# Pair 5 of the MLP with seven products, two more kept items at heads 14 to 16, and the odd tile's conv ahead of the last gate step

## The chip, the cores and the metric

The kernel runs on one core of a Trainium2 chip. The metric is device time in microseconds, the median of three runs; lower is better. Profiles are of one further execution, whose own time stands beside its span, since the span counts from the first to the last instruction only.

The engines are TensorE (PE; its weight loads are listed apart as PEld), VectorE (DVE), ScalarE (ACT), GpSimd (POOL) and SyncE (SP, which here only issues DMAs). Each takes its instructions in a fixed order and waits at one whose input is not there yet.

## The reference

One layer of a decoder trunk on 512 rows of 1024 in fp32: attention with forget gates (16 heads of 64), layernorm, a gated MLP with a causal three-tap convolution on the gate, layernorm, and a gated per-layer embedding.

```
mix = fox_mixer(x, w_in, b_f, w_out)          # 16 heads, scores + c_q - c_k, softmax, w_out
x = layer_norm(ALPHA * x + mix, g, b)
u, g = split(x @ w_up, [2816])                # 1024 -> 2 x 2816
g = causal_dwconv(g, conv_w, conv_b)          # 3 taps along the sequence
x = layer_norm(ALPHA * x + (gelu(g) * u) @ w_down, g2, b2)
x = x + sigmoid(x @ w_gate + b_gate) * (p @ w_proj)
```

## The kernel before

**Products.** Every fp32 product is three matmuls of a rounded type (`three`, L152): high part times high part, high times low, low times high. Activations and weights are cut into these parts: ACT makes `whi` (L123), DVE makes `wlo` as the difference (L129). Weights come in units of 512 KB (128 x 1024) through SyncE's queue into `raw`, a ring of four buffers; the parts are five deep.

**Attention.** A loop over h runs scores of head h, transposes of the probabilities of head h − 1 (`turn`) and values of head h − 2 (`values`: L593 on PE, then ACT L599 and DVE L600 write `o`; behind an odd head ACT L602 and DVE L603 make the parts `oh` and `ol`). The output product starts early: `out_first(k)` adds row block k into the banks `ao`, for half of the columns, and the other half goes into the banks `ap` after the loop. A scheduler sets the order on each engine here, by its own estimate of times.

**Layernorm.** For each of four row tiles DVE adds `ao` and `ap` to `y` (L689), takes statistics and normalizes (L705, L706); PE transposes the result (`nt`, L714).

**MLP.** The 22 column tiles f of the up product are taken in pairs j = 0 to 10 (f = 2j and 2j + 1), gate g and value u of each. A plain tile takes 24 matmuls of 512 columns for g and 24 for u. In the pairs of `UP_PAIRS` the 2 x 2 block product is done with seven half-size products instead of eight (Strassen's scheme in Winograd's form): `up_step` has four stages, with 24, 24, 24 and 12 matmuls of 256 columns for each of g and u. The stages collect in `E`, from which the convolution (`conv`: ACT, then two DVE operations), gelu and the product with u follow. Between the steps of a pair the down product of an earlier part runs in pieces (`between`). In the MLP the order on DVE and ACT is the order in which the code is written (`manual_schedule`); an instruction that waits holds up what stands behind it there.

**Kept sums.** A seven-product pair needs sums of weight blocks. For the pairs in `KEPT` they are made during attention: `keep_load` (L478) loads two 512 KB pieces, `ka` into a buffer of its own (one only) and `kb` into the ring `raw`; `keep_sums` (L489 to L492, four DVE subtractions) makes the sums in place; the next `keep_load` stores them to DRAM (`kept`, L472) before it loads the next item. One item is one side (u or g) of one pair: eight items for the four pairs. From `kept` the MLP loads them like weights.

**Operands.** The sums and parts of a pair's result, which the down product reads, are made at the pair's end or, for a pair whose successor is in `APART`, inside the successor's first step (`operand_sums`, L885 to L888; `operand_parts`, L893 and L894).

Of the kernel before, what the change touches and what calls it, by code (L numbers as in the profile page):

```python
# [17 lines left out]
S = 512  # L18
D = 1024
H = 16  # L20
# [10 lines left out]

CHUNKS = (None, (1,) * 12, (1,) * 12, (2, 1) * 4)

UP_PAIRS = (2, 3, 4, 6, 7, 9)

KEPT = (3, 4, 6, 7)

DMA_PAIRS = (1, 2)

APART = (2, 3, 4, 7)  # L40
HALF = S // 2
ALPHA = 2.0 ** 0.25
EPS = 1e-5
# [99 lines left out]
def trunk_layer(ctx: ExitStack, tc: tile.TileContext, xT, x2d, pT, w0, wqk, wv1, wv2, bf, wo, wup, cwb,  # L143
# [323 lines left out]
    def keep_load():  # L467

        if made:
            to, ab = made.pop()  # L470
            for n, t in enumerate(ab):
                nc.sync.dma_start(to[:, 2 * n:2 * n + 2, :], t.rearrange("p (a b) -> p a b", b=512))  # L472
        if to_keep:
            (j, q), to = to_keep.pop(0)
            ab = (ap.tile([P, UNIT], F32, name=f"ka{j}_{q}", tag="keep", bufs=1),
                  base.tile([P, UNIT], F32, name=f"kb{j}_{q}", tag="raw", bufs=RAW_BUFS))
            for n, t in enumerate(ab):
                nc.sync.dma_start(t.rearrange("p (a b) -> p a b", b=P), wup[2 * j + n, 1 - q])  # L478
            in_work.append((to, ab))
# [166 lines left out]
    for h in range(H + 2):  # L646
        m, s = divmod(h, 2)
        if h == 2:
            project(2, 0)
        if h < H:  # L650
            scores(h)

            if s == 0 and h != 2:
                keep_sums()
                keep_load()
        if m + 1 < KD and h != 2:
            project(m + 1, s)
        for k in OUT_FIRST.get(h, ()):
            out_first(k)
        if s == 1 and h + 1 < H:  # L660
            stack(h + 1)
        if 1 <= h < H + 1:
            turn(h - 1)
        if h >= 2:
            values(h - 2)
        if s == 1 and h + 1 < H:
            stack(h + 2)
        if h == H:
            y = base.tile([P, NT, D], F32, tag="xh", name="y")
            for t in range(NT):  # L670
                nc.sync.dma_start(y[:, t, :], x2d[t * P:(t + 1) * P, :])
# [113 lines left out]
    def conv(f):  # L785

        pg = ups.pop((f, 0))
        a = gates[f] = hpool.tile([P, S], F32, tag="a", name=f"a{f}", bufs=2)
        nc.scalar.activation(a, pg, AF.Identity, bias=cw[:, f, 3:4], scale=cw[:, f, 2:3])
        nc.vector.scalar_tensor_tensor(a[:, 1:], pg[:, :S - 1], cw[:, f, 1:2], a[:, 1:],  # L790
                                       op0=ALU.mult, op1=ALU.add)
        nc.vector.scalar_tensor_tensor(a[:, 2:], pg[:, :S - 2], cw[:, f, 0:1], a[:, 2:],
                                       op0=ALU.mult, op1=ALU.add)

    def product(f, e):
        a = gates[f]
        nc.scalar.activation(a, a, AF.Gelu)
        nc.vector.tensor_mul(e, gates.pop(f), ups.pop((f, 1)))
# [67 lines left out]
            del ups[j, s]  # L866
            nc.scalar.activation(e[:, HALF:S], x, AF.Copy)

    def conv_product(fs, E):

        for f in fs:
            c = slice(f % 2 * S, f % 2 * S + S)
            ups[f, 0], ups[f, 1] = E[:, 2 * S:][:, c], E[:, c]
            conv(f)
        for f in fs:
            product(f, E[:, f % 2 * S:f % 2 * S + S])

    def operand_sums(E):

# [63 lines left out]
    for part in range(4):  # L943
        ops = []
        slots = iter(CHUNKS[part] or ())

        def between():
            for _ in range(next(slots, 0)):
                next(before)

        for f in range(6 * part, min(6 * part + 6, NF)):
            q, j = f % 2, f // 2
            if f >= 6:
                next(beside)
            if f == 2:

                ordered.enter_context(tc.manual_schedule(
                    engines={mybir.EngineType.DVE, mybir.EngineType.Activation}))
            if q == 0 and j not in APART:
                E = hpool.tile([P, 8 * HALF], F32, tag="E", name=f"E{j}")  # L960
            if f == 0:
                a, b = slice(0, HALF), slice(HALF, S)
                up(0, 0, a)
                up(0, 1, a)
                up(1, 0, a, (3, x1h, x1l, xt))
                up(0, 0, b)
                up(0, 1, b)
                up(1, 0, b)
                conv(0)
                product(0, E[:, :S])  # L970
                continue
            if j in UP_PAIRS:
                if q == 0:
                    up_step(j, 0, 0, E)
                    between()
                    up_step(j, 0, 1, E, (lambda: operand_sums(E)) if j in APART else None)
                    if j in APART:
                        operand_parts(pending.pop(), E)
                        E = hpool.tile([P, 8 * HALF], F32, tag="E", name=f"E{j}")
                    between()  # L980
                    continue
                for st in (1, 2):
                    up_step(j, st, 0, E)
                    up_step(j, st, 1, E)
                    if st == 1:
                        between()
                between()
                up_step(j, 3, 0, E)
                up_step(j, 3, 1, E)
                conv_product((f, f - 1), E)  # L990
            else:
                if f > 1:
                    up(f, 0)

                n = 4 * (j - 3 * part) + 2 * q
                late = part and any(sum(CHUNKS[part][:n], i) % 3 == 2 for i in range(CHUNKS[part][n]))
                if not late:
                    conv(f)
                between()
                if late:  # L1000
                    conv(f)
                up(f, 1)
                product(f, E[:, q * S:(q + 1) * S])
            if f == 1:
                x_sums()
            if q:
                if part < 3:
                    ops.append([cut_tiles("A", 2, 3, f"a{j}"), cut_tiles("B", 1, 5, f"b{j}", pool=hpool),
                                cut_tiles("S", 4, 4, f"s{j}")])
                    if j + 1 in APART:  # L1010
                        pending.append(ops[-1])
                    else:
                        operand_sums(E)
                        operand_parts(ops[-1], E)
                else:
                    h, l = cut_tiles("S", 4, 4, f"s{j}")
                    e = E[:, :2 * S].rearrange("p (a b) -> p a b", b=HALF)
                    last_cut[:] = [nc.scalar.activation(h, e, AF.Copy).ins]
                    nc.vector.tensor_sub(l, e, h.bitcast(F32))
                    ops.append((h, l))  # L1020
            if j not in UP_PAIRS:
                between()
        if part < 3:
            before = down(part, ops)
# [216 lines left out]
```

## Time and profile before

| | before |
|---|---|
| time, median of 3 runs | 646.02 us (645.39 to 646.28) |
| profiled execution | 645.37 us, span 643.5 us, granted clock 1.000 |
| PE, PEld | 638.3 us (99%), 560.6 us (87%) |
| DVE | 532.4 us (83%) |
| ACT | 383.4 us (60%) |
| POOL | 127.6 us (20%) |
| moved by DMA | 121.08 MB, mean 188 GB/s |

By stage, the end of attention runs from about 196 to 222 us, the first layernorm to about 254, pairs 2 to 5 of the MLP end at about 311.9, 343.0, 374.1 and 403.0 us, pair 9 at 530.6. "Busy" is time in which an instruction runs on the engine; the chain that ended last is the sequence of instructions, followed back from the last one, each of which released the next.

### The profile page before, as it was taken

To read this page: it belongs to the slowest core of one execution; us is meant where nothing else is said; L and a number is where in the kernel's file an instruction comes from. 1 tells how busy PE (TensorE), PEld (TensorE's weight loads), DVE (VectorE), ACT (ScalarE), POOL (GpSimd) and SP (SyncE) were. 2 spreads that over 40 slices of the span, in tenths; PEclk is the share of its full clock that TensorE was granted. 3 is DMA by queue.
4 is the path that set the end of the run, shared out by engine and by line. 5 is a ranking of instruction groups with operands and counts; after the bars stand their busy time and mean duration, and the time that the engine had idled before them with its cause. 6 is when DMAs were issued, how large, how long until landed. Compare 5 with 4: busy or idle time off the path is not lost.

```text
span 643.5 us, 10085 instructions
## 1 busy us (share of the span) xinstructions
PE 638.3 (99%) x3635; PEld 560.6 (87%) x3635; DVE 532.4 (83%) x863; ACT 383.4 (60%) x682; POOL 127.6 (20%) x147
## 2 busy tenths in 40 slices
PE   9999999999999999999999999999999999999997
PEld 7899888888888889989999988999988998888886
DVE  6576778988888599857899987889897998699997
ACT  6274777877785326945757563647555455336872
POOL 2000554454456043110000010101011001002001
PEclk9999999999999999999999999999999999999999
DMA  8763625454588387684676838765746764782732
GB/s 314 249 226 117 209 80 185 160 189 155 177 272 321 129 256 215 135 215 156 202 221 158 227 125 250 192 205 149 238 132 202 193 217 115 164 276 61 232 109 98
DMA packets 49393, 121.08 MB, mean 188 GB/s; under 512 B 4864, under 2 KB 7936, under 8 KB 49344
## 3 DMA queue, kind: packets, MB, share of 16 engines
q1 hardware_dynamic: 44400, 107.21, 49.8%
q0 software_dynamic: 4800, 13.11, 11.0%
q8 instruction: 28, 0.46, 0.3%
q14 instruction: 21, 0.17, 0.1%
q10 hardware_dynamic: 144, 0.13, 0.1%
HBM read 107.72 MB, written 18.87 MB: 197 GB/s over the span
## 4 chain that ended last, share of the span: by engine, by line
PE 97%; DMA 1%; DVE 1%; ACT 0%; issue 0%; SPq 0%; DVEq 0%
PE g L152 18%; PE u L152 18%; PE pp L152 14%; PE x L152 8%; PE pv L152 7%; PE pl L152 7%; PE z L152 4%; PE r L152 3%; PE ap L152 3%; PE o L593 3%; PE t L580 2%; PE ao L152 2%; PE y L152 2%; PE s L543 2%; PE s L545 2%; DMA y<-x2d 1%
## 5 line engine op out<-in xcount | busy, mean ns | idle before, releaser
L123 ACT ACTIVATE whi<-raw 128x1024 fp32r<-128x1024 f32 (+4 forms) x136 | 128.1, 945 | 95.0 <-PE pv L152 17.9
L129 DVE TENSOR_TENSOR wlo<-raw,whi 128x1024 fp32r<-128x1024 f32 (+4 forms) x131 | 140.0, 1076 | 27.9 <-ACT whi L123 27.2
L567 POOL TENSOR_SCALAR pr<-pr,rl 128x128 f32<-128x128 f32 (+1 forms) x64 | 75.5, 1194 | 128.1 <-DVE rl L563 125.6
L281 POOL COPY neghalf<-neghalf 128x1 f32<-128x1 f32 x16 | 9.0, 563 | 247.1 <-ACT neghalf L280 247.1
L152 PE MATMUL g<-x1h,whi 128*128 128x256 f32 (+1 forms) x168 | 54.7, 325 | 0.0
L152 PE MATMUL g<-x1l,whi 128*128 128x256 f32 (+1 forms) x168 | 54.4, 324 | 0.0
L152 PE MATMUL g<-x1h,wlo 128*128 128x256 f32 (+1 forms) x168 | 54.3, 324 | 0.0
L152 PE MATMUL u<-x1l,whi 128*128 128x256 f32 (+1 forms) x160 | 52.9, 331 | 0.0
L152 PE MATMUL u<-x1h,wlo 128*128 128x256 f32 (+1 forms) x160 | 52.9, 331 | 0.0
L152 PE MATMUL u<-x1h,whi 128*128 128x256 f32 (+1 forms) x160 | 52.9, 331 | 0.0
L152 PE MATMUL pp<-xh,whi 128*128 128x512 f32 (+1 forms) x130 | 50.7, 390 | 0.0
L152 PE MATMUL pp<-xl,whi 128*128 128x512 f32 (+1 forms) x130 | 50.7, 390 | 0.0
L152 PE MATMUL pp<-xh,wlo 128*128 128x512 f32 (+1 forms) x130 | 50.5, 390 | 0.0
L559 ACT ACTIVATE pr<-s,nm 128x128 f32<-128x128 f32 (+1 forms) x64 | 33.5, 527 | 9.1 <-DVE nm L555 8.9
L152 PEld LDWEIGHTS g<-x1h,whi 128*128 128x128 f32 x168 | 31.9, 190 | 3.4 <-issue 0.7
L152 PEld LDWEIGHTS g<-x1l,whi 128*128 128x128 f32 x168 | 31.9, 190 | 2.7
L152 PEld LDWEIGHTS g<-x1h,wlo 128*128 128x128 f32 x168 | 31.9, 190 | 2.6
L152 PEld LDWEIGHTS u<-x1l,whi 128*128 128x128 f32 x160 | 30.4, 190 | 3.0
L152 PEld LDWEIGHTS u<-x1h,whi 128*128 128x128 f32 x160 | 30.4, 190 | 3.0
L152 PEld LDWEIGHTS u<-x1h,wlo 128*128 128x128 f32 x160 | 30.4, 190 | 2.8
L123 ACT ACTIVATE whi<-side 128x512 fp32r<-128x512 f32 (+1 forms) x33 | 25.5, 782 | 10.4 <-PE u L152 3.6
L555 DVE CUSTOM_DVE_ANT_0 s<-s,mask 128x128 f32<-128x128 f32 (+1 forms) x64 | 30.1, 510 | 1.7 <-PE s L545 1.5
(636 smaller groups left out, 1870.9 us busy)
## 6 DMA issues: line engine op xcount, KB each, us to landing
raw<-wup SPq DMA_DIRECT2D x34, 512.0 KB, 9.1
raw<-wdn SPq DMA_DIRECT2D x23, 512.0 KB, 6.7
raw<-wqk SPq DMA_DIRECT2D x14, 512.0 KB, 5.8
ka<-wup SPq DMA_DIRECT2D x8, 512.0 KB
kb<-wup SPq DMA_DIRECT2D x8, 512.0 KB, 4.3
kept<-kb SPq DMA_DIRECT2D x8, 512.0 KB, 3.2
kept<-ka SPq DMA_DIRECT2D x8, 512.0 KB
raw<-wo SPq DMA_DIRECT2D x8, 512.0 KB, 4.9
```

What stands on the lines that cost most here:

```text
L123: self.nc.scalar.activation(hi[:, c:e], piece, AF.Copy)
L129: self.nc.vector.tensor_sub(lo[:, c:e], piece, hi[:, c:e].bitcast(F32))
L152: nc.tensor.matmul(ps, lhsT, rhs, start=start and n == 0, stop=stop and n == 2, skip_group_check=on)
L281: with tc.issue_after(nc.gpsimd.tensor_copy(small[:, m + 32:m + 33], small[:, m:m + 1]).ins):
L543: nc.tensor.matmul(ps[:, :n], QA[:, q], KA[:, :n], start=True, stop=False)
L545: nc.tensor.matmul(ps[:, :n], qb[0:68, q], kb[0:68, :n], start=False, stop=True)
L555: last_mask[:] = [nc.vector.tensor_tensor_reduce(ps[:, :w], ps[:, :w], mask[:, S - w:], -1.0, BIG, op0=ALU.add, op1=ALU.min, accum_out=nm[ ...
L559: nc.scalar.activation(pr[:, off:off + w], ps[:, :w], AF.Exp, bias=nm[:, i:i + 1], scale=-1.0, accum_out=ls[:, i:i + 1])
L567: nc.gpsimd.tensor_scalar_mul(pr[:, off:off + w], pr[:, off:off + w], rl[:, i:i + 1])
L580: nc.tensor.transpose(ps[:, w:w + P], pr[:, o:o + P], ident)
L593: nc.tensor.matmul(ps[:, q0:], V[:, j, h], p[:, o:o + w], start=j == 0 and n == 0, stop=j == NT - 1 and n == 1)
```

## The change

Pair 5 becomes a seven-product pair and a kept one: with it the pairs 2 to 7 are consecutive. Pairs 5 and 6 join `APART`, so that the operand sums and parts of pairs 4 and 5 are made inside the first step of pairs 5 and 6. Ten items are now kept; the calls that were made at h = 14 and before are joined by one pair of calls at h = 15 and one at h = 16, so that pair 7's two sides come last, behind pair 5's and 6's. And in every seven-product pair the function that did conv of both tiles and then the product of both is split: the odd tile's conv is written ahead of the gate's last step, its product behind it, then comes the value's last step, then conv and product of the even tile.

```diff
-UP_PAIRS = (2, 3, 4, 6, 7, 9)
-KEPT = (3, 4, 6, 7)
+UP_PAIRS = (2, 3, 4, 5, 6, 7, 9)
+KEPT = (3, 4, 5, 6, 7)
-APART = (2, 3, 4, 7)
+APART = (2, 3, 4, 5, 6, 7)
@@ the loop over h
-            if s == 0 and h != 2:
+            if s == 0 and h != 2 or h == H - 1:
                 keep_sums()
                 keep_load()
+        elif s == 0:
+            keep_sums()
+            keep_load()
@@
-    def conv_product(fs, E):
-        for f in fs:
-            c = slice(f % 2 * S, f % 2 * S + S)
-            ups[f, 0], ups[f, 1] = E[:, 2 * S:][:, c], E[:, c]
-            conv(f)
-        for f in fs:
-            product(f, E[:, f % 2 * S:f % 2 * S + S])
+    def conv_of(f, E):
+        c = slice(f % 2 * S, f % 2 * S + S)
+        ups[f, 0], ups[f, 1] = E[:, 2 * S:][:, c], E[:, c]
+        conv(f)
+    def product_of(f, E):
+        product(f, E[:, f % 2 * S:f % 2 * S + S])
@@ the end of a seven-product pair
                 between()
+                conv_of(f, E)
                 up_step(j, 3, 0, E)
+                product_of(f, E)
                 up_step(j, 3, 1, E)
-                conv_product((f, f - 1), E)
+                conv_of(f - 1, E)
+                product_of(f - 1, E)
```

The lines below L650 move down by three. On DVE, at the end of attention (`o_2241` and `o_2381` are the outputs of the last two pairs of heads, `PTl` low parts of probabilities), there stood before:

```order
343 L600 TENSOR_TENSOR o_2241<-o_2322,o_2241 64x512
344 L603 TENSOR_TENSOR ol<-o_2241,oh 128x512
345 L584 TENSOR_TENSOR PTl_396<-t_0_2353,PTh_394 128x512
346 L584 TENSOR_TENSOR PTl_396<-t_1_2360,PTh_394 128x384
347 L584 TENSOR_TENSOR PTl_396<-t_3_2366,PTh_394 128x384
348 L600 TENSOR_TENSOR o_2381<-o_2372,o_2381 64x512
349 L129 TENSOR_TENSOR wlo_2514<-raw_2405,whi_2513 128x1024
350 L600 TENSOR_TENSOR o_2381<-o_2419,o_2381 64x512
```

And now (`ka_0`, `kb_0` are the item of pair 7's side 0, `ka_1`, `kb_1` that of side 1; the two outputs are named `o_2247` and `o_2403`):

```order
342 L489 TENSOR_TENSOR ka_0_2181<-kb_0_2182,ka_0_2181 128x512
343 L600 TENSOR_TENSOR o_2247<-o_2338,o_2247 64x512
344 L490 TENSOR_TENSOR kb_0_2182<-kb_0_2182 128x512
345 L129 TENSOR_TENSOR wlo_2524<-raw_2361,whi_2523 128x1024
346 L491 TENSOR_TENSOR kb_0_2182<-kb_0_2182,ka_0_2181 128x512
347 L603 TENSOR_TENSOR ol<-o_2247,oh 128x512
348 L492 TENSOR_TENSOR ka_0_2181<-ka_0_2181,kb_0_2182 128x512
...
352 L600 TENSOR_TENSOR o_2403<-o_2394,o_2403 64x512
353 L129 TENSOR_TENSOR wlo_2536<-raw_2427,whi_2535 128x1024
354 L489 TENSOR_TENSOR ka_1_2285<-kb_1_2286,ka_1_2285 128x512
355 L600 TENSOR_TENSOR o_2403<-o_2441,o_2403 64x512
```

The sums of two items are woven into the last heads, and the first sum of the last item stands directly ahead of the last L600. On SyncE there stood before, from the last stores of kept sums to the layernorm's rows:

```order
126 L472 DMA kept_1_70<-kb_1_1967 128x1024
127 L472 DMA kept_1_70<-ka_1_1966 128x1024
128 L93 DMA raw_2493<-wup 128x1024
129 L93 DMA raw_2505<-wup 128x1024
...
134 L93 DMA raw_2529<-wup 128x1024
135 L683 DMA cw<-cwb 128x88
136 L679 DMA g_2456<-gm 128x1024
```

And now:

```order
127 L472 DMA kept_1_70<-ka_1_1968 128x1024
128 L93 DMA side<-wup 128x1024
129 L93 DMA raw_2361<-wo 128x2x512
130 L478 DMA ka_0_2181<-wup 128x1024
...
135 L472 DMA kept_0_71<-ka_0_2181 128x1024
136 L472 DMA kept_0_71<-kb_0_2182 128x1024
137 L478 DMA ka_1_2285<-wup 128x1024
138 L93 DMA raw_2527<-wup 128x1024
139 L93 DMA raw_2539<-wup 128x1024
140 L472 DMA kept_1_72<-kb_1_2286 128x1024
141 L472 DMA kept_1_72<-ka_1_2285 128x1024
```

The two further items bring two loads of `ka` and four stores into this stretch (their `kb` loads stand further ahead), in front of the layernorm's rows. On ACT, at the end of a seven-product pair (here pair 2; `E` collects the stages, `a` is the convolution, L789 its start and L797 the gelu), there stood before:

```order
315 L867 ACTIVATE E_3228<-g_3147 128x256
316 L123 ACTIVATE whi_3376<-raw_3267 128x1024
317 L867 ACTIVATE E_3228<-u_3183 128x256
318 L789 ACTIVATE a_3396<-E_3228,cw 128x512
319 L789 ACTIVATE a_3400<-E_3228,cw 128x512
320 L797 ACTIVATE a_3396<-a_3396 128x512
321 L797 ACTIVATE a_3400<-a_3400 128x512
```

And now:

```order
314 L792 ACTIVATE a_3379<-E_3250,cw 128x512
315 L123 ACTIVATE whi_3383<-raw_3256 128x1024
316 L870 ACTIVATE E_3250<-g_3169 128x256
317 L800 ACTIVATE a_3379<-a_3379 128x512
318 L123 ACTIVATE whi_3404<-raw_3289 128x1024
319 L870 ACTIVATE E_3250<-u_3205 128x256
320 L792 ACTIVATE a_3424<-E_3250,cw 128x512
321 L800 ACTIVATE a_3424<-a_3424 128x512
```

The odd tile's convolution starts ahead of the copies of the last step, its gelu between the two, and only the even tile's stand behind.

## The prediction

> **What bounds the kernel now.** I read the page first: busy shares, then the chain that ended last.
>
> ```profile
> span 643.5 us, 10085 instructions
> PE 638.3 (99%) x3635; PEld 560.6 (87%) x3635; DVE 532.4 (83%) x863; ACT 383.4 (60%) x682; POOL 127.6 (20%) x147
> PE 97%; DMA 1%; DVE 1%; ACT 0%; issue 0%; SPq 0%; DVEq 0%
> ```
>
> TensorE (PE) is busy 638.3 of 643.5 us, and the chain runs 97% through its matmuls. So time is saved only by fewer or shorter matmuls, and lost wherever a matmul is made to wait. Where the second could happen is read from the busy times by stage (columns: stretch and its length; busy us and count of PE, PEld, DVE, ACT, POOL; granted clock; DMA share; GB/s).
>
> ```profile
> 343.00:374.10 31.10, 31.10 (x217) 29.14 (x217) 27.78 (x39) 19.24 (x34) 2.43 (x4) 1.00 0.74 198
> 374.10:403.00 28.90, 28.90 (x129) 23.63 (x128) 23.34 (x35) 14.39 (x23) 3.06 (x4) 1.00 0.62 179
> 494.00:530.60 36.60, 36.60 (x242) 33.68 (x241) 36.00 (x55) 20.17 (x35) 2.22 (x4) 1.00 0.65 190
> 196.00:222.00 26.00, 25.93 (x138) 21.89 (x137) 15.66 (x29) 12.09 (x26) 9.93 (x8) 1.00 0.60 215
> 222.00:246.00 24.00, 24.00 (x119) 20.09 (x119) 22.13 (x33) 8.32 (x12) 10.47 (x19) 1.00 0.75 227
> ```
>
> The first three are MLP blocks: pair 4 (seven products), pair 5 (plain), pair 9 (seven products). PE is full in each, at clock 1.00, and pair 9 shows that it stays full with DVE busy 36.00 of 36.60 us. The fourth is the end of attention, where DVE has 10 us free and which the new kept sums enter; the fifth is the first layernorm, where DVE is busy 22.13 of 24.00 and can take little.
>
> **The change, part 1: fewer matmul columns (pair 5).** The pieces of the chain give PE's price of each kind of step.
>
> ```profile
> 379.57 1.36 PE x L152 x6
> 382.30 5.44 PE u L152 x24
> 297.47 2.88 PE g L152 x24
> 308.99 1.44 PE g L152 x12
> ```
>
> A plain tile of u or g is 24 matmuls of 512 columns, 5.44 us; a plain pair has four, 21.76 us. A seven-product pair has per side three steps of 24 matmuls of 256 columns, 2.88 us, and a last one of 12, 1.44 us: 6 × 2.88 + 2 × 1.44 = 20.16 us. Pair 5 therefore gives back **1.60 us**, and since PE has no gap there nothing dilutes it. The pitches are 5.44/24 = 227 ns and 2.88/24 = 120 ns. The Trainium skill ("TensorE: Matmul & The Clock Gate", section "Wait — 56ns, not 53.3ns?") has a warm matmul start every N/2.4 GHz plus 2.5 ns, measured on another type. By that rule, as an estimate, the 96 matmuls would cost 96 × 215.8 ns and the 168 would cost 168 × 109.2 ns, a saving of 2.4 us instead of 1.6. The trace's pitches lie 11 ns above the rule at both widths, and a fixed excess counts 168 against 96 times; the measurement decides.
>
> **Part 2: DVE in pair 5's block.** The block shrinks to 20.16 us plus its five down steps of 1.36 us, 27.0 us. Its DVE work is read from pair 4, of the same kind but with eight down steps ((31.10 − 20.16)/1.36): 27.78 us, less for three steps at least the low part of the down weight.
>
> ```profile
> L129 DVE TENSOR_TENSOR wlo<-raw,whi 128x512 fp32r<-128x512 f32 x26 | 17.8, 686 | 3.0 <-ACT whi L123 2.8
> ```
>
> That is 27.78 − 3 × 0.69 = 25.7 us in 27.0, 95%, below pair 9's 98%. I cost it at nothing; its cover is the weights cut ahead, and if that is used up the loss is at most what DVE has over: I bound it at 0.5 us. A gain here is excluded, PE having no gap. The kept sums of pair 5 are not in it, being made in attention.
>
> **Part 3: conv and product of the odd tile, ahead of and behind the gate's last step.** DVE and ACT follow their written order. The odd tile's conv and gelu now run beside the last 2.88 us of a seven-product pair instead of after it, so that three fewer instructions of some 0.7 us stand on DVE ahead of the next pair's operands. What waits behind the moved conv is the E copy of the gate's last step, on ACT, which only the even tile's conv needs. PE waits for neither. Cost and gain: zero, for want of any PE gap.
>
> **Part 4: two more kept sums at the end of attention.** This is where I expect a loss. Only one `ka` buffer exists, so the two new items go in a chain: store of pair 7's predecessor lands, load of (7,0), its sums, its store lands, load of (7,1), its sums. And DVE's order puts the last item's first sum (L489) ahead of the last head's L600, on which the attention output rests. SyncE's issues, and the DMAs' times to landing:
>
> ```profile
> 179.38 0.33 SPq L472 DMA_DIRECT2D kept<-ka  x1
> 181.89 0.39 SPq L93 DMA_DIRECT2D raw<-wo  x1
> 183.02 0.35 SPq L478 DMA_DIRECT2D ka<-wup  x1
> 196.59 0.33 SPq L472 DMA_DIRECT2D kept<-kb  x1
> 198.53 0.33 SPq L472 DMA_DIRECT2D kept<-ka  x1
> 198.94 3.09 SPq L93 DMA_DIRECT2D raw<-wup  x2
> 221.96 0.33 SPq L683 DMA_DIRECT2D cw<-cwb  x1
> ...
> kept<-kb SPq DMA_DIRECT2D x8, 512.0 KB, 3.2
> raw<-wo SPq DMA_DIRECT2D x8, 512.0 KB, 4.9
> ...
> raw<-wo SPq DMA_DIRECT2D x2, 512.0 KB, 4.0
> ...
> raw<-wo SPq DMA_DIRECT2D x1, 512.0 KB, 5.7
> ```
>
> The last two rows are of the stretches 143 to 149 and 178 to 184 us. Stores: 3.2 us (median). The one of 179.38 took 3.6: SyncE had finished issuing at 182.28 and sent the next `ka` load, which needs that store, only at 183.02. The `kb` store of 196.59 took 5.1: the second of the two loads at 198.94 waits for it and went out at 198.94 + 3.09 − 0.33 = 201.7. Loads of the same size: 4.0 to 5.7. DVE and the two engines that hang on it at the end of attention:
>
> ```profile
> 195.12 0.66 DVE L490 TENSOR_TENSOR kb<-kb 128x512 f32<-128x512 f32 x1
> 197.62 0.88 DVE L492 TENSOR_TENSOR ka<-ka,kb 128x512 f32<-128x512 f32 x1
> 219.73 0.68 DVE L600 TENSOR_TENSOR o<-o,o 64x512 f32<-64x512 f32 x1 [2.54 <-ACT o L599]
> 221.12 0.69 DVE L603 TENSOR_TENSOR ol<-o,oh 128x512 fp32r<-128x512 f32 x1 [0.70 <-ACT oh L602]
> 222.62 1.28 DVE L689 SCALAR_TENSOR_TENSOR y<-y,ao 128x512 f32<-128x512 f32 x2 [0.81 <-PE ao L152]
> 228.53 0.68 DVE L689 SCALAR_TENSOR_TENSOR y<-y,ap 128x512 f32<-128x512 f32 x1
> 236.73 1.29 DVE L706 SCALAR_TENSOR_TENSOR y<-y,mv,b 128x1024 f32<-128x1024 f32 x1 [0.47 <-POOL mv L702]
> 251.65 1.27 DVE L706 SCALAR_TENSOR_TENSOR y<-y,mv,b 128x1024 f32<-128x1024 f32 x1
> ...
> 220.45 0.63 ACT L602 ACTIVATE oh<-o 128x512 fp32r<-128x512 f32 x1 [0.75 <-DVE o L600]
> ...
> 221.19 0.91 PE L152 MATMUL ao<-whi,oh 128*128 128x512 f32 x3
> 253.38 1.04 PE L714 MATMUL nt<-ident,y 128*128 128x128 f32 x8
> ```
>
> In numbers: the store of 198.53, in the same crowd as the 5.1, lands about 202.5. The load of (7,0) takes 4.9, to 207.4. DVE then stands as the order shows: four sums, an L600, a weight's low part of 1.2 us and an L603, 5.3 us together, to 212.7. The store (between 3.2 and 3.6; nothing else is sent then but its twin behind it) with 0.3 for the issue: 216.2. The load of (7,1) I take at **3.6 us**, between the quiet 3.2 of a store of this size and the 4.0: landing at L = 219.8. From there one sum (0.6) and what follows L600 today, 219.73 to the matmul at 221.19 or 1.46: `oh` is ready at L + 2.1. PE has one more `ap` matmul of 227 ns ahead, so it asks at 221.4. Its wait is L − 219.3 = **0.5 us**; 0 with an early landing, 1.7 with stores of 3.6 and a load of 4.4.
>
> Next late: DVE. From L it has L489, L600, L490, L491, L603 and L492, some 3.9 us, then what lies today from 222.62 to 228.53, 5.9 us: L + 9.8 = 229.6 against 228.53, 1.1 us late. The row at 221.96 is late too: the new last `ka` store is ahead of it on SyncE, and the layernorm's tiles lie where `ka` lay, so that they start when it has landed, near 223.7 + 3.2 + 0.3 = 227.2, with the last of them there some 6 us later, about when the late DVE asks; I add 0.2. Against these 1.3 us stand 0.46 us at the end (y of the last tile ready at 251.65 + 1.27 = 252.92, asked for at 253.38), the 0.47 us that DVE waits for POOL in the second tile and may now fill, and the 0.5 us that PE itself is late. What is left is **0.1 us**; bounds 0 and 1.0. No gain can hide in this part: PE busy 25.93 of 26.00.
>
> **Sum**: −1.60 + 0 + 0 + 0.5 + 0.1 = −1.0 us. The profiled execution took 645.37 us, 1.9 more than its span, and lies at the low end of the runs (median 646.02). On its own scale the change gives 644.4; on the median 645.0.
>
> **Rivals.** What can be told from no change is about 0.2%, 1.3 us.
>
> A, *the whole 1.6 us arrives*: the last load lands by 219.3, half a microsecond sooner than I have it, or DVE reaches the sum later than L600's input anyway. For it: in my chain every transfer but the last two is priced from crowded stretches. Against it: six links in a row would all have to be at their shorter ends. Median 644.4.
>
> B, *slower*: the chain of kept items lands late. With the 5.1 of the store at 196.59 and the load of 5.7 in place of 3.2 and 3.6, L is 212.7 + 5.1 + 0.3 + 5.7 = 223.8, PE stands 4.5 us at the last head, the layernorm's rows come as much later, and the time is 646.02 − 1.6 + 4.5 + 0.5 = 649.4. It decides from L = 222.2, where 2.9 us of stall leave +1.3. For it: three transfers of 512 KB through one buffer in sequence, in the order on SyncE's one queue, with weight loads between them. Against it: the crowd of 196 to 202 was of six transfers at once; at 213 to 220 today only one load is sent.
>
> C, *DVE bounds pairs 5 and 6*: 95% busy and in a fixed order, a matmul waits for a low part of a weight or for an operand. For it: kept pairs need all their weights cut in the same 27 us. Against it: pairs 3, 4 and 9, as dense, show PE full. It costs up to 0.5 in each of two blocks: about 646.0, no difference.
>
> D, *the saving is that of the rule, 2.4 us*: 256-column matmuls would have to come closer than 120 ns apart in pair 5, though 297.47 and 308.99 show 120 in pair 3. With the 0.6 of stalls: 644.2. The page is the Trainium skill's on TensorE, named above.
>
> **How the numbers follow.** Chances: my forecast (stall 0.2 to 1.2) 0.42; A 0.20; between my forecast and B (stall 1.2 to 2.9) 0.13; B 0.12; C 0.10; D 0.03. Faster than 644.7 is A, D and the lower part of my own, 0.38 together; slower than 647.3 is B, 0.12, and a trace of C; the rest, 0.49, is within. The range goes from 643.9 (the whole saving with the runs at their low end, 645.39 − 1.6 = 643.8) to 646.9, where 2.5 us of stalls leave +0.9; B lies outside.
>
> **What would show it.** In the changed profile: pair 5 as six pieces of 2.88 and two of 1.44 us, PE busy lower by 1.6 us; PE with a gap of half a microsecond ahead of the first `ao` matmuls of the last head, put down to ACT's `oh`, and DVE's L489 of the last item idle before it on a DMA; a second, smaller one at the transposes `nt`. Full steps in the MLP, with DVE over 93% in pair 5. I would be wrong if L489 does not wait (A), if the gap is over 3 us (B), if matmuls in pairs 5 or 6 stand on `wlo` or on an operand (C), or if an instruction that I count as covered, an exponential of head 15 behind the moved weight cut on ACT, say, makes PE wait before 209.

## The result, and the profile after

The changed kernel takes **650.16 us** (median of 4 runs, 649.99 to 650.37) against 646.0: a ratio of 1.0066, interval 1.0053 to 1.0079. It is slower by 4.2 us where 1.0 us less was forecast. Its profiled execution took 650.13 us, with a span of 648.2. From the page of its profile, busy times and the chain that ended last:

```profile
span 648.2 us, 10283 instructions
PE 639.7 (99%) x3707; PEld 565.1 (87%) x3707; DVE 541.3 (84%) x879; ACT 390.4 (60%) x700; POOL 128.6 (20%) x147
PE 80%; DVE 10%; DMA 6%; issue 2%; POOL 1%; ACT 1%; DVEq 0%; ACTq 0%; POOLq 0%
```

PE was 97% of the chain and is 80%: DVE and DMA now carry 16% of it, although PE's share of busy time still reads 99%. (The chain is followed back through whatever was waited for, so these 16% are not the size of the loss.) PE's busy time even rose by 1.4 us with cheaper matmuls in pair 5. Both point to matmuls that wait or run slowly. By windows (columns as in the prediction):

```profile
221.00:224.00 3.00, 1.09 (x5) 0.60 (x4) 2.25 (x4) 0.63 (x1) 0.00 (x0) 1.00 0.80 298
225.40:228.60 3.20, 3.20 (x10) 2.49 (x9) 1.86 (x4) 0.00 (x0) 0.00 (x0) 0.55 0.81 319
379.20:407.07 27.87, 27.42 (x200) 25.79 (x198) 23.21 (x36) 17.43 (x32) 2.48 (x4) 1.00 0.73 220
```

The first row is the last head: PE is idle for two thirds of it. The second, just behind, is full, but at a granted clock of 0.55, with only ten matmuls in 3.2 us; that is why "busy" went up. The third is pair 5, with a gap. The rows behind the first two, from the timelines of SyncE, DVE, ACT and PE:

```profile
214.08 0.33 SPq L472 DMA_DIRECT2D kept<-ka  x1
218.13 0.33 SPq L478 DMA_DIRECT2D ka<-wup  x1
225.74 0.33 SPq L472 DMA_DIRECT2D kept<-ka  x1
230.64 0.33 SPq L686 DMA_DIRECT2D cw<-cwb  x1
...
208.98 0.69 DVE L489 TENSOR_TENSOR ka<-kb,ka 128x512 f32<-128x512 f32 x1 [1.14 <-DMA ka<-wup]
221.65 0.69 DVE L489 TENSOR_TENSOR ka<-kb,ka 128x512 f32<-128x512 f32 x1 [4.16 <-DMA ka<-wup]
222.37 0.69 DVE L600 TENSOR_TENSOR o<-o,o 64x512 f32<-64x512 f32 x1
...
223.09 0.63 ACT L602 ACTIVATE oh<-o 128x512 fp32r<-128x512 f32 x1 [3.11 <-DVE o L600]
...
223.78 1.21 PE L152 MATMUL ao<-whi,oh 128*128 128x512 f32 x4 [1.91 <-ACT oh L602]
224.82 0.58 PE L152 MATMUL ap<-wlo,oh 128*128 128x512 f32 x1
228.70 0.40 PE L152 MATMUL ap<-whi,ol 128*128 128x512 f32 x1
250.06 1.09 PE L717 MATMUL nt<-ident,y 128*128 128x128 f32 x8 [0.56 <-DVE y L709]
```

The wait is the one that the prediction named: DVE stands 4.16 us at the last item's first sum, for the load of `ka`; L600 stands behind it; PE waits for `oh`. Counted from the pitch of 227 ns, up to the start of the next matmul, it loses 2.07 us there. From 224.82 to 228.70 it issues ten matmuls of 512 columns, which take 2.27 us at that pitch, in 3.88: another 1.6 us go to the slow clock. At the end of the layernorm it loses 0.72 us, and attention up to the last head ran 0.3 us longer. Together these are 4.7 of the 4.8 us by which the first matmul of the MLP is late:

```profile
250.91 0.36 PE L152 MATMUL g<-x1h,whi 128*128 128x256 f32 x1
569.03 0.39 PE L152 MATMUL r<-whi,s9h 128*128 128x512 f32 x1
```

Before, these two stood at 246.11 and 564.42. From the one to the other, which I call the MLP below, it was 318.31 us and is 318.12: of the 1.60 us of pair 5, 0.19 is left. The other 1.4 us are PE's waits, by the pitch about 0.7 us in pair 5 (ahead of the `g` matmul at 407.07), 0.4 in pair 7 (ahead of `x` at 455.60) and 0.35 at the transposes `nt` of the last row tile (258.53), which stand behind the first matmuls of the MLP and did not wait before.

### The profile page after: what moved, and what is told of

Read it like the earlier page. It is cut to its first block, busy times and chain, and to the rows that moved or that the text cites. A ratio compares the mean times of both kernels' runs of the same rounds, so it can differ in the third digit from the quotient of the medians.

```text
span 648.2 us, 10283 instructions
## 1 busy us (share of the span) xinstructions
PE 639.7 (99%) x3707; PEld 565.1 (87%) x3707; DVE 541.3 (84%) x879; ACT 390.4 (60%) x700; POOL 128.6 (20%) x147
## 4 chain that ended last, share of the span: by engine, by line
PE 80%; DVE 10%; DMA 6%; issue 2%; POOL 1%; ACT 1%; DVEq 0%; ACTq 0%; POOLq 0%
PE g L152 14%; PE u L152 14%; PE pp L152 14%; PE pv L152 7%; PE pl L152 7%; PE x L152 6%; PE r L152 3%; PE z L152 3%; DVE wlo L129 2%; PE o L593 2%; DMA kept<-ka 2%; PE t L580 2%; PE y L152 2%; PE s L543 2%; DMA ka<-wup 1%
## 5 line engine op out<-in xcount | busy, mean ns | idle before, releaser
L129 DVE TENSOR_TENSOR wlo<-raw,whi 128x1024 fp32r<-128x1024 f32 (+4 forms) x134 | 143.1, 1076 | 22.4 <-ACT whi L123 21.4
L152 PE MATMUL g<-x1h,whi 128*128 128x256 f32 (+1 forms) x164 | 51.7, 315 | 0.5 <-ACT E L870 0.5
L152 PE MATMUL g<-x1l,whi 128*128 128x256 f32 (+1 forms) x164 | 51.6, 315 | 0.0
L152 PE MATMUL g<-x1h,wlo 128*128 128x256 f32 (+1 forms) x164 | 51.5, 314 | 0.0
L152 PE MATMUL u<-x1l,whi 128*128 128x256 f32 (+1 forms) x156 | 50.1, 321 | 0.0
L152 PE MATMUL u<-x1h,wlo 128*128 128x256 f32 (+1 forms) x156 | 50.1, 321 | 0.0
L152 PE MATMUL u<-x1h,whi 128*128 128x256 f32 (+1 forms) x156 | 50.1, 321 | 0.0
L152 PE MATMUL u<-xsh,whi 128*128 128x256 f32 x112 | 31.7, 283 | 0.0
L152 PE MATMUL g<-xsh,wlo 128*128 128x256 f32 x112 | 31.7, 283 | 0.0
L152 PE MATMUL u<-xsl,whi 128*128 128x256 f32 x112 | 31.7, 283 | 0.0
```

Of the source, the lines that this page charges most:

```text
L129: self.nc.vector.tensor_sub(lo[:, c:e], piece, hi[:, c:e].bitcast(F32))
L152: nc.tensor.matmul(ps, lhsT, rhs, start=start and n == 0, stop=stop and n == 2, skip_group_check=on)
```

## The experiments

In the table, "MLP begins" is the start of that first `g` matmul in the profiled execution and "MLP" the time from it to the first `r` matmul, both from PE's timeline. Times are medians, each with its ratio to runs of the kernel before on the same chip (645.6 to 645.9 there).

| kernel | time, us | ratio (interval) | MLP begins | MLP |
|---|---|---|---|---|
| before | 646.0 | | 246.1 | 318.3 |
| changed | 650.2 | 1.0066 (1.0053 to 1.0079) | 250.9 | 318.1 |
| two more kept items alone | 650.0 | 1.0062 (1.0048 to 1.0076) | 251.9 | 318.8 |
| conv split alone | 645.7 | 0.9994 (0.9986 to 1.0003) | 246.1 | 317.8 |
| changed, PE filled at the last head | 651.3 | 1.0084 (1.0071 to 1.0097) | 251.2 | 317.4 |
| changed, items one head earlier | 647.1 | 1.0013 (1.0003 to 1.0024) | 248.0 | 318.7 |
| changed, items spread | 649.2 | 1.0054 (1.0042 to 1.0065) | 251.9 | 317.5 |
| spread, copy first | 650.3 | 1.0075 (1.0063 to 1.0087) | 249.4 | 320.3 |
| spread, old APART | 650.3 | 1.0070 (1.0057 to 1.0082) | 250.4 | 319.1 |
| pair 5 in place of 7 | 647.2 | 1.0030 (1.0018 to 1.0042) | 246.2 | 320.0 |
| ... less DVE | 645.6 | 0.9995 (0.9986 to 1.0005) | 246.6 | 317.8 |
| ... POOL's transfers moved | 645.2 | 0.9989 (0.9979 to 0.9999) | 246.2 | 317.9 |
| changed, last `ka` in the ring | 646.4 | 1.0000 (0.9989 to 1.0011) | 248.0 | 317.6 |
| before, transfers moved | 645.7 | 1.0002 (0.9992 to 1.0012) | 246.0 | 318.3 |
| changed, transfers moved | 647.6 | 1.0041 (1.0026 to 1.0055) | 248.8 | 317.2 |
| ring, transfers moved | 645.4 | 0.9996 (0.9986 to 1.0005) | 246.7 | 318.3 |
| ring, transfers and gate copies moved | **644.1** | 0.9975 (0.9966 to 0.9983) | 246.4 | 316.4 |
| before, transfers and gate copies moved | 645.6 | 0.9999 (0.9990 to 1.0008) | 246.5 | 318.3 |

**The two kept items alone.** The kernel before, with

```diff
-KEPT = (3, 4, 6, 7)
+KEPT = (3, 4, 5, 6, 7)
-            if s == 0 and h != 2:
+            if s == 0 and h != 2 or h == H - 1:
                 keep_sums()
                 keep_load()
+        elif s == 0:
+            keep_sums()
+            keep_load()
```

> The kernel before with only the two more kept items (pair 5's sums are made and stored and never read; pair 5 stays plain, the conv order stays). Theory T (the loss sits at the end of attention: the last item's sum waits for its load and holds the last head's L600, PE idles some 2 us, runs slow behind it and stands once more in the layernorm): 646.0 + 5.0 = 651.0, with the idle of 2 us and a granted clock near 0.55 behind it as in the changed kernel. Rival M (the loss sits in the MLP's denser blocks 5 and 6): 646.0.

650.0 us, where T had 651.0. The windows of its last head, of the stretch behind it and of the layernorm's end:

```profile
221.00:224.50 3.50, 1.26 (x6) 0.72 (x5) 2.42 (x4) 0.63 (x1) 0.00 (x0) 1.00 0.86 318
226.00:229.00 3.00, 3.00 (x9) 2.35 (x8) 1.67 (x4) 0.01 (x1) 0.00 (x0) 0.58 0.83 313
249.00:252.00 3.00, 1.77 (x13) 1.31 (x12) 2.54 (x4) 0.99 (x2) 1.47 (x3) 1.00 0.90 205
```

The idle time, the slow clock and the late layernorm are all there without a single change in the MLP. By the pitch PE waits 2.40 us at the last head and 1.38 at the end of the layernorm. Theory T holds in its mechanism: the loss up to the MLP is the price of the two kept items at the end of attention.

**The conv split alone.** `conv_product` replaced as in the diff of the change, nothing else.

> The kernel before with only the conv and product of the odd tile moved ahead of and behind the gate's last step, in its six seven-product pairs. Theory T: 646.0, no PE gap added. Rival O (the conv and gelu on ACT, ahead of the copy of the gate's last step, keep its bank from the next pair): 646.5 to 647.5, with PE waiting for the E copy at the ends of pairs 3 and 6.

645.7, no difference; rival O falls. In pair 2 the steps stay at 2.88 and 1.44 us. That part is free.

**Filling PE's idle time.** The changed kernel with the first `ap` tile's work on the seven finished row blocks ahead of the last head's (cut: `ap_rows` repeats the loop that stands behind `out_first(7)`, and that loop now does only the eighth block of this tile):

```diff
+    ap0 = bank("ap0")
+    ap_rows(0, ap0, range(KD - 1))
     out_first(7)
 ...
```

> The changed kernel with ten more matmuls of the ap product (2.3 us) put ahead of the last head's ao matmuls on PE; DVE's and SyncE's orders stay. Both theories expect the idle of 2.07 us to shrink to 0 to 0.2 and the clock to stay at 1.00, which saves 3.7 us at that place. Theory G (the layernorm's rows g and b, sent only when the last kept store has landed, set the end of the layernorm by themselves): the 0.72 us stall there grows to 4 to 4.5, the time stays at 649.7 to 650.2. Rival H (the last head's stall and the slow clock are the whole loss): 646.4.

651.3: it gains nothing. Its windows at the last head, and DVE and PE in the layernorm:

```profile
221.00:224.00 3.00, 2.64 (x12) 1.87 (x10) 2.90 (x5) 0.63 (x1) 0.00 (x0) 1.00 0.48 187
225.40:228.60 3.20, 3.20 (x16) 2.63 (x15) 2.48 (x4) 1.06 (x1) 0.00 (x0) 1.00 0.78 273
...
229.82 0.69 DVE L699 BATCH_NORM_STATS2 st<-y 128x6 f32<-128x512 f32 x1 [1.94 <-DMA kept<-ka]
...
238.31 1.06 PE L717 MATMUL nt<-ident,y 128*128 128x128 f32 x8 [1.85 <-DVE y L709]
```

Sixteen matmuls now run where ten ran, at a clock of 1.00; 0.9 us of idle time are left at the last head, and the MLP still begins at 251.2, since PE now waits 2.0 and 2.5 us at the transposes of the layernorm. DVE waits for the landing of the last kept store before it can write its first statistics, since these tiles lie where the kept buffer lay. Rival H falls. Theory G is right that the stall moves to the layernorm and grows to 4.5 us there, and wrong about what is waited for: the statistics, not the rows g and b. Its range ended at 650.2; the profiled execution took 649.7, the median is above. The last head and the layernorm are two waits on one chain, in parallel, and to hide the first only brings out the second.

**The chain moved.** First one head earlier, with head 2's slot used, then spread to one and a half heads between three of the items. The cut shows the first; in both the calls at `elif s == 0` fall away, and the sums at head 15 are put behind the low parts of the probabilities. The spread one calls at heads 0, 4, 6, 8, 11 and 14 in the first place and at 9, 12 and 15 in the second:

```diff
-            if s == 0 and h != 2 or h == H - 1:
+            if s == 0:
 ...
             turn(h - 1)
+            if h == H - 1:
+                keep_sums()
+                keep_load()
```

> The changed kernel with the kept items moved up: the slot at head 2 is used, the calls at head 16 fall away, and the last item's sums stand behind the low parts of the probabilities at head 15. Theory T: no idle at the last head, the layernorm as before, and what is left is the MLP's saving as the changed kernel shows it (1.6 less some 1.0 of stalls): 645.4, 644.9 to 645.9. Rival C (the chain of kept items is late wherever it lies, since the stores and loads crowd the weights): 647.5 or more, with PE waiting near 208 us.

> The changed kernel with the ten kept items spread so that three of them follow each other after one and a half heads instead of two (early in heads 0, 4, 6, 8, 11, 14, late in heads 9, 12, 15) and head 2 left free; the last sums again stand in head 15. Theory T: no idle at the last head, no stall in heads 2 and 3 (1.0 us near 88 us in the variant that used head 2), what is left is the MLP's 1.6 us less its stalls: 645.2 to 646.0. Rival C (a chain of items at one and a half heads is late too): 647 or more, with PE waiting in heads 9 to 15.

647.1 and 649.2. The first has no idle time at the last head, as T said, but begins the MLP at 248.0: it pays 1.0 us near 88 us, where PE waits for DVE, and its MLP has the stalls of pair 5 in full. The spread one loses more than it mends: PE waits 1.7 us in head 12 (up to 172.83), 0.75 in head 14 (up to 192.49) and 1.7 in head 15, the last of them here:

```profile
204.64 0.39 PE L543 MATMUL s<-KA,QA 128*128 128x256 f32 x1 [1.58 <-DVE PTl L584]
```

T's number is missed in both, and rival C is right for the spread one: neither place that was tried is cheap for ten items with one `ka` buffer.

**Pair 5 without the tail.** Pair 5 takes the place of pair 7, so that eight items are kept as before (`APART` loses pair 7 too, and the calls at heads 15 and 16 fall away).

```diff
-UP_PAIRS = (2, 3, 4, 5, 6, 7, 9)
+UP_PAIRS = (2, 3, 4, 5, 6, 9)
-KEPT = (3, 4, 5, 6, 7)
+KEPT = (3, 4, 5, 6)
```

> The changed kernel with pair 7 plain and not kept: pairs 2 to 6 and 9 have seven products, eight items are kept at the same heads as before, so the end of attention is as before. As many matmuls as before. Theory T: attention ends without a stall, the stalls of 0.6 to 1.0 us at the end of pair 5 stay: 646.4 to 647.0. Rival A (the stalls in the MLP follow from the late end of attention): 645.8 to 646.0, no stall in pairs 5 and 6.

647.2, slightly more than T had: attention ends as before, and the MLP is 1.7 us longer for the same number of matmuls. So rival A falls: the stalls in the MLP do not need a late end of attention. PE waits twice in pair 5, 1.1 and 1.0 us by the pitch with the slower first matmul behind each wait:

```profile
383.68 0.50 PE L152 MATMUL x<-whi,b0h 128*128 128x512 f32 x1 [0.85 <-DVE y L691]
403.18 0.39 PE L152 MATMUL g<-x1h,whi 128*128 128x256 f32 x1 [0.70 <-ACT E L867]
...
397.76 1.06 ACT L123 ACTIVATE whi<-raw 128x1024 fp32r<-128x1024 f32 x1 [3.57 <-DMA raw<-wup]
401.80 1.06 ACT L123 ACTIVATE whi<-raw 128x1024 fp32r<-128x1024 f32 x1 [0.30 <-DMA raw<-wup]
402.76 0.37 ACT L867 ACTIVATE E<-g 128x256 f32<-128x256 f32 x1
```

The first is for DVE's additions to `y`; the second for ACT's copy of the gate's bank, which stands behind two cuts of weights that land late. Here is the same place as the chain of waits of the changed kernel has it (start, duration, what):

```profile
396.81 0.69 DVE wlo L129
...
397.52 8.06 DMA raw<-wup
...
405.69 1.06 ACT whi L123
406.75 0.28 ACT E L870
...
407.07 0.51 PE g L152 x2
```

A load of a weight goes out when DVE's cut frees the ring, takes 8.06 us, and ACT's cut, the copy and PE follow from it.

**Two attempts on the order.** On the spread variant: ACT's copy of the gate's last step ahead of the next weight cut, and pairs 5 and 6 out of `APART`.

```diff
-        hi, lo = W.get(u_up[j, st, s], 4)
+        hi, lo = W.get(u_up[j, st, s], 3 if st == 3 and s == 0 else 4)
 ...
             nc.scalar.activation(e[:, HALF:S], x, AF.Copy)
+            W.get(u_up[j, st, s], 4)
```

> The spread variant with one more edit: at the last step of each seven-product pair's gate, ACT copies the bank before it cuts the next weight. Theory E (the 0.6 us in which PE waits at the end of pair 5 comes from that copy standing behind a weight whose load is late): 0.6 us under the spread variant. Rival D (DVE is late as a whole and the wait moves on): within 0.2 us of it.

> The spread variant with pairs 5 and 6 out of APART, so that the operand sums and parts of pairs 4 and 5 are made at those pairs' ends again. Theory P (those operands, made inside the first step of pairs 5 and 6, hold up the weight cuts there, so that the ring comes free late and loads go out in bursts): the stalls of pairs 5 and 6 go, 1.0 us less. Rival D (DVE has no room in these blocks wherever the work stands): the same or slower by up to 1 us.

650.3 and 650.3, with an MLP of 320.3 and 319.1 us. Theories E and P both fall: with the copy first, ACT waits 2.10 us at another cut for another load, and stalls appear in pairs 4 to 7; with the old APART, PE waits 1.3 us behind the first step of pair 5 and 0.8 in pair 6. Neither reordering helps.

**Two causes taken away.** On the variant with pair 5 in place of 7: the two DVE operations of the convolution left out in four tiles, or POOL's three adding transfers moved out of pairs 4 and 5.

```diff
+        if f in (8, 9, 10, 11):
+            return
```
```diff
-            if f >= 6:
+            for _ in range(0 if f in (9, 10, 11) else 2 if f in (19, 20, 21) else f >= 6):
                 next(beside)
```

> The variant with pair 5 in place of pair 7, with the two DVE operations of the convolution left out in the four tiles of pairs 4 and 5 (those tiles miss two taps): 3 us less on DVE in each of the two blocks, nothing else. Theory D (DVE is late in pair 5's block, frees the ring late, and so weights land late and banks come free late): the stalls of 2.1 us in pair 5 shrink under 0.5 and the time falls to 645.2 to 645.9. Rival Q (the DMA queues, with POOL's adding transfers for the gate, are too slow there): 647 as that variant.

> The variant with pair 5 in place of pair 7, with the three adding transfers of POOL that fall into pairs 4 and 5 (tiles 9 to 11) made in tiles 19 to 21 instead. Rival Q: loads of weights in pair 5 land in 4 to 6 us instead of 6 to 9, its stalls of 2.1 us mostly go: 645.5 to 646. Theory D: the loads are sent in the same burst, the time stays at 646.8 to 647.3.

645.6 and 645.2: either edit alone takes away all of the stalls, with an MLP of 317.8 and 317.9 us against 320.0. The loads of `raw<-wup` in the two variants, and the one for which ACT waited before, from SyncE's timeline: sent at 391.06 with the transfers and all of DVE's work, at 388.76 with less DVE work, at 389.97 without the transfers:

```profile
391.06 0.33 SPq L93 DMA_DIRECT2D raw<-wup  x1
```
```profile
388.76 0.33 SPq L93 DMA_DIRECT2D raw<-wup  x1
```
```profile
389.97 0.33 SPq L93 DMA_DIRECT2D raw<-wup  x1
```

And the issue, size and time to landing of POOL's transfer in the variant with both, among the DMAs of 388 to 398 us:

```profile
gt<-gt POOLq DMA_DIRECT2D x1, 256.0 KB, 5.8
```

It is sent at 390.25, just ahead of that load. ACT can cut the load's weight at 397.76, 6.7 us after it was sent; in the other two ACT no longer waits for it. So D and Q are both half right: a late DVE lets the burst of loads out late (six in 4.0 us from 391.06 on; with less DVE work six in 4.3 us, but 2.3 us sooner), and POOL's transfer lies across that burst. Each takes the slack of the other; with one of them gone PE waits no more.

**The buffer.** The changed kernel, with the very last `ka` in the ring of four, so that its load waits for no store:

```diff
-            ab = (ap.tile([P, UNIT], F32, name=f"ka{j}_{q}", tag="keep", bufs=1),
+            ab = (ap.tile([P, UNIT], F32, name=f"ka{j}_{q}", tag="keep", bufs=1) if to_keep else
+                  base.tile([P, UNIT], F32, name=f"ka{j}_{q}", tag="raw", bufs=RAW_BUFS),
```

> The changed kernel with one edit: the `ka` piece of the very last kept item lies in the ring of four like its `kb`, not in the one `keep` buffer, so that its load waits for no store and the layernorm's tiles wait for the store before it. Theory T (one buffer makes a chain of store, load, sums, store, which ends too late for the last head and for the layernorm): no idle at the last head, granted clock 1.00, layernorm as before; 4.5 us under the changed kernel, 645.4 to 646.2. Rival B (DVE and the ring have no room at the end of attention, whoever owns the buffer): 648 or more, with PE waiting on a weight cut from the ring between 205 and 226 us.

646.4, 3.7 us under the changed kernel and level with before: T holds, the single buffer makes the chain, though T's range ended at 646.2. 1.9 us of the MLP's late begin are left, 0.5 near 211 us and 1.3 at the end of the layernorm, where DVE waited 2.54 us for POOL's small operation (L706).

**The rest.**

```diff
-        for _ in range(2 if t < 3 else 0):
+        for _ in range(2 if t else 0):
             copies.send(st[:, 1, :1])
```

> The kernel before with the three adding transfers of POOL of tiles 9 to 11 made in tiles 19 to 21. Theory S (they cost something only where a seven-product pair 5 stands, since only there loads go out in a burst with no slack): 645.9, no difference. Rival (they cost PE time in any case): 645.3 or less.

> The changed kernel with the last item's `ka` in the ring and POOL's three adding transfers moved to tiles 19 to 21. Theory S (the MLP's saving is 1.6 us once the loads of pair 5 are not held up): the stalls in pairs 5 and 7 under 0.3 together, against 0.7; the layernorm's stalls of 1.3 and 0.3 stay: 645.6 to 646.1. Rival D (DVE alone is late): as with the ring alone, 646.4.

> The same, with the copies of the gate's weights that POOL sends behind each row tile of the layernorm begun one tile later, so that the second tile's power on POOL stands ahead of two of them. Theory L (DVE waited 2.5 us for that power, which stood behind two transfers that POOL could not send yet): the stall of 1.3 us at the end of the layernorm goes, 644.5 to 645.0, faster than before. Rival W (the layernorm is late because its rows are): no difference to the kernel without this edit.

> The kernel before (pair 5 plain, eight kept items) with both moves of POOL's transfers: tiles 9 to 11 made in 19 to 21, and the gate's copies begun one row tile later. Theory S (the gain of the last variant is pair 5's): 645.5 to 645.9, no difference. Rival (it is POOL's): 644.1 to 644.5.

> The changed kernel with only the three adding transfers moved. Theory S: the tail of attention keeps its 4.7 us, the MLP gains some 0.7 to 1.0: 649.2 to 649.6. Rival (they hardly matter here): 650.0 to 650.3.

The ring with the transfers moved takes 645.4, better than S had; its profiled execution has no stall in pair 5, but 1.3 us of them in pair 7, which S did not expect and which I leave unexplained. With the gate's copies one tile later it is **644.1**, faster than both kernels by more than the uncertainty. POOL's rows and DVE's in the second row tile, without that edit and with it:

```profile
234.78 0.73 POOL L272 DMA_DIRECT2D gt<-wg  x1 [2.31 <-issue]
237.45 0.58 POOL L706 TENSOR_TENSOR mv<-mv,neghalf 128x1 f32<-128x1 f32 x1
238.07 1.28 DVE L710 SCALAR_TENSOR_TENSOR y<-y,mv,b 128x1024 f32<-128x1024 f32 x1 [1.47 <-POOL mv L706]
```
```profile
236.29 0.71 POOL L706 TENSOR_TENSOR mv<-mv,neghalf 128x1 f32<-128x1 f32 x1
237.03 1.28 DVE L710 SCALAR_TENSOR_TENSOR y<-y,mv,b 128x1024 f32<-128x1024 f32 x1 [0.46 <-POOL mv L706]
```

L is supported in its mechanism: the operation no longer stands behind a transfer that POOL cannot send. Its share is not settled: 0.3 us of the 1.2 between the two show where the MLP begins, another 0.35 at the last row tile's transposes; the rest is in the stalls of pair 7 that one execution had and the other had not. What the final kernel shows from the page is plain:

```profile
PE 636.8 (99%) x3707; PEld 563.6 (88%) x3707; DVE 541.4 (84%) x879; ACT 390.2 (61%) x700; POOL 127.6 (20%) x147
PE 99%; DVE 0%; issue 0%; DVEq 0%
```

PE is 99% of the chain, its busy time 1.5 us under that of before, and the time 1.5 us under: the 1.60 us of the matmuls, arrived. The same moves on the kernel before do nothing (645.7 with the transfers, 645.6 with both), so that the gain is pair 5's. (The kernel before with its last `ka` in the ring was not run; it has no wait at the last head to lose.) The changed kernel with the transfers moved gains 2.6 us by the medians where S expected 0.6 to 1.0; by the ratios it is 1.6, and its six runs spread from 647.0 to 650.6. Its MLP is shorter by 0.9 as expected. For the other part I have only an observation, and a telling one: in its profiled execution, with the same code in attention, the last load landed 2.1 us sooner.

```profile
219.57 0.69 DVE L489 TENSOR_TENSOR ka<-kb,ka 128x512 f32<-128x512 f32 x1 [2.33 <-DMA ka<-wup]
```

PE then waits 0.24 us at the last head, and 2.3 us in two places in the layernorm; the MLP still begins 2.7 us late. That the landing differs by chance between executions is not shown: the four runs of the changed kernel itself lie within 0.4 us.

## Why the prediction was wrong, step by step

**Right:** that PE is the bound and pair 5's matmuls save 1.60 us (the pitches of 120 ns held in pair 5, and the final kernel shows the sum; the rule of the Trainium skill, "TensorE: Matmul & The Clock Gate", section "Wait — 56ns, not 53.3ns?", with its 2.4 us is not what came); that the conv split is free; where the loss would sit, which instruction waits for which, and that the wait is L − 219.3. With L = 221.65 that gives 2.35 against a measured 2.07, with 219.57 it gives 0.27 against 0.24.

**The landing L** was the mis-sized term at the last head: 219.8 put down, 221.65 measured. The first sum of the first item began at 208.98 instead of 207.4, its store went out at 214.08 instead of 212.7, and from there to the next load it took 4.05 us instead of 3.5. The load (5.9 us) and the store (4.0) were each somewhat longer than the 4.0 to 5.7 and 3.2 to 3.6 that I had allowed. In four profiled executions with the same code there, L was 219.6, 220.9, 221.7 and 222.0: the one number that I put down is a spread of 2.4 us, on a chain of transfers through one queue, and its late end costs more than its early end saves.

**The clock** was not a term of the sum at all: every duration in it is one at a granted clock of 1.00. Behind its wait PE lost another 1.6 us to the granted clock. No row that the prediction shows from the profile before has such a wait; but the price of a stall was then not bounded from above, and the text treated it as its length.

**The layernorm, "0.1 us; bounds 0 and 1.0"**, is the step that failed most. I had only `cw`, g and b behind the last kept store; DVE's statistics are behind it as well, and POOL's transfers and small operation behind those. With PE late by 3.7 us it shows as 0.72, and 0.35 more at the last row tile; with PE nearly in time it is 2.3 (the changed kernel with the transfers moved) or, with PE filled, 4.5. In the one profiled execution with an early landing the MLP therefore still begins 2.7 us late, more than pair 5 saves: as far as that execution shows, my own case and rival A could not come true. The two waits had to be taken as alternatives, each with its own end, and not as one with a remainder.

**Pair 5's DVE, "95%, below pair 9's 98%"**, costed at nothing: PE lost 1.1 us in the blocks of pairs 5 and 7 beyond what it lost before, about 0.7 of it in pair 5, where I had bounded it at 0.5. The share of DVE was not the measure: in pair 5's window DVE was busy 23.21 of 27.87 us, 83%, and PE waited all the same. What counted was how long DVE's cuts kept the ring from SyncE, and which other transfer lay across the burst of loads. Pair 9 has no such burst: its six closest loads go out over 8.6 us in the kernel before, against 4.0. Rival C named the right engine and about the right price (up to 0.5 in each of two blocks), but not what is waited for: a copy on ACT behind a late load, and DVE's additions to `y`.

**Rival B**, the slower case, comes nearest with 649.4, but by another account: a stall of 4.5 us in it, against 2.07 of stall, 1.6 of clock, 0.72 of layernorm, 0.3 ahead and 1.4 of the 1.6 us lost again in the MLP. I gave it 0.12, since each of its links was at its far end; the links that I left out made up for that.

## What to carry to other kernels

Work that is put into free time of an off-path engine is not free if it is the last on a chain of load, compute, store through one buffer: follow that chain to its end, and then to everything that takes over its memory. Where two consumers wait on the same late transfer, cost each as if the other were not there; hiding one brings out the other. And a stall on a full TensorE is to be priced above its length where the clock may follow it down: here 2.07 us of waiting cost 3.7.

## What the runs showed of the hardware that was not expected

After 2.07 us without a matmul, TensorE ran four matmuls at a granted clock of 1.00 and then 3.4 us, from 224.87 to 228.29, at 0.50 (the row 225.40 to 228.60 above reaches past its end, hence the mean of 0.55): 512 columns took 427 ns instead of 227. After 2.4 us idle in the kernel with only the kept items it was the same (225.09 to 228.51). Idle times of 1.9 and 2.0 us in the layernorm, in the changed kernel with the transfers moved and in the filled one, left the clock at 1.00, and so did the 2.5 us ahead of 250.36 in the filled one. The Trainium skill ("TensorE: Matmul & The Clock Gate", section "Why this matters for your kernels") asks for no idle gap over some 3 us. These runs show a drop after less than that, and not after every gap of the same length; the same page's description of a free-running window of 3.4 us (section "What's actually happening") would fit a drop that depends on when the gap falls. The clock record of these traces agrees: in the changed kernel the full clock before the drop lasts 218.45 us and the drop 3.413, that is 64 steps and one. Cut at these steps, the gap of 2.07 us lies whole in one step (221.46 to 224.87), and so does that of 2.4; the filled kernel's gap of 2.5 us, cut at its own steps, falls into two (1.7 us up to 249.56 and 0.8 behind). The gaps of 1.9 and 2.0 us lie whole in one step too and brought no drop, so that the place alone does not decide; no run varied the gap by itself, and five gaps are too few for a rule.

POOL's adding transfer of 256 KB took 5.5 to 5.8 us, and loads of 512 KB sent within a few us of it up to 8.06; the page of the changed kernel has a median of 3.8 for its 31 loads of `raw<-wup`. How much of this is the adding transfer is not isolated: with pair 5 in place of 7 and the transfers moved away, a load sent 2.6 us behind the burst (`raw<-kept`) still took 6.3, and the kernel before has a median of 9.1 for the same loads.
